# A layer of three mixers on one core: the attention's turn is given out in two parts, scores ahead of the heads' steps, values and transposes behind them

## The chip, the cores and the metric

The kernel runs on one core of a Trainium2 chip. The core has five engines with a queue of instructions each: TensorE (PE, matmuls and transposes, with a sequence of weight loads of its own, PEld), VectorE (DVE), ScalarE (ACT), GpSimd (POOL) and SyncE (SP, which issues DMAs). Operands lie in the on-chip memory SBUF, and results of matmuls in the accumulator memory PSUM. The metric is the device time of one execution in microseconds (us), less is better.

## The reference

One layer of a hybrid decoder trunk on 1024 positions of width 1024 in float32: a projection into three groups of columns, a mixer for each group, an output projection, then a gated MLP with a short convolution, a gated embedding and a last norm.

```python
z = rmsnorm(h, norm_mix_g[l]) @ w_in[l]
a_q, a_f, a_i, a_g, b_q, b_k, b_v, c_in = jnp.split(z, splits, axis=-1)
o_a = hgrn2_mix(a_q, a_f, a_i, a_g, lbs[l], hgrn_gnorm_g[l])
o_b = dilated_window_mix(b_q, b_k, b_v)
...
o_c, v_first = rwkv7_mix(c_in, ...)
h = h + jnp.concatenate([o_a, o_b, o_c], axis=-1) @ w_out[l]
h = h + conv_glu_ffn(rmsnorm(h, norm_ffn_g[l]), ...)
gate = jax.nn.sigmoid(rmsnorm(h, norm_ple_g[l]) @ ple_gate[l])
h = h + gate * (p[l] @ ple_proj[l])
```

Two of the mixers matter here. HGRN2 has four heads of 128 columns; in chunks of 64 positions it computes, for each head,

```python
o_inter = jnp.einsum('bhck,bhkv->bhcv', qc * jnp.exp(b), state)
scores = jnp.einsum('bhik,bhjk,bhijk->bhij', qc, kc, jnp.exp(rel))
o_intra = jnp.einsum('bhij,bhjv->bhiv', scores, vc)
state = (jnp.exp(b_last[:, :, 0, :])[..., None] * state
         + jnp.einsum('bhck,bhcv->bhkv', kc * jnp.exp(b_last - b), vc))
```

and norms the output per head. The attention has four heads of 64 columns and mixes three causal windows (128 positions, 512 with a stride of 4, 2048 with a stride of 16) by their softmax denominators; in the kernel that is one softmax over all earlier positions, with a mask that is added to the scores.

## The kernel before

The program is written stage by stage: norm and projection, RWKV-7, then the stage of this case with HGRN2 and the attention together, then the output projection, the MLP, the gated embedding and the last norm. In this stage several streams of work are Python generators. `phase_mix` (L321 to 341) writes an order as a list of letters, and `interleave` (L66) gives each letter's stream a turn up to its next `yield`:

- A and B are the HGRN heads. `handover` (L75) runs head 0 and then head 2 in A, head 1 and then head 3 in B. B starts six rounds after A.
- C is the attention, `swa` (L1110). It has a turn in the rounds of `TURNS`, two of three: 1, 3, 4, 6, 7, 9, 10, and so on to 33.
- F is `project_late` (L462): halves of the projections that are still due, 24 matmuls each (zp, L137 to 141), up to round 22, then the splitting of finished outputs into two parts for the output projection (L160, L162). It has a turn in the rounds of `LATE`: 1, 4, 7, 10, 13, 16, 19, 22 and then 23 to 28.
- M are 24 further pieces ahead of the first round.

One round is C, A, B, F, as far as each has a turn in it. A program that builds the kernel then arranges the instructions of each engine by readiness, with the written order as priority. So the written order is not quite the order on an engine. Engines wait for one another by semaphores.

A step of a head (`hgrn_head`, L950 to 1108): the head's inputs are loaded and prepared (L964 zl, L967 hk, L969 qt), own scores are made (L989), then come seven levels. A level is one step: 16 small matmuls (hsc, L1015) on the keys that ACT copied (ks, L1002); DVE copies them masked into hS (COPY_PREDICATED, L1017); keys and queries are multiplied by a factor (hk, L1026, on POOL in odd levels and DVE in even ones; qt, L1028, on DVE). The next level's matmuls need that qt and the next ks. After the levels come transposes of values and keys (vt, L1043 and L1049; ACT copies them to hV and hkt, L1044 and L1050), states (hkv, L1064, hst, L1071 and L1073), outputs (hpo, L1083 and L1085; ACT copies them to ho, L1086), the norm (square on ACT, hsq, L1090; sum on DVE, hss, L1092; power on POOL, hrs, L1095; product on DVE, ho, L1097), and transposes of the output (vt, L1103) with the gate (zl, L1104).

A turn of the attention handles one block of 128 queries (q block) of two heads. There are two pairs p of heads, of 8 q blocks each, and ten turns a pair, since the work is staggered:

- `swa_out` (L1215): after every fourth q block, the reciprocal denominators are spread by 16 matmuls (swd, L204) and the output ob multiplied (L1220);
- `swa_scores` (L1158) of q block qb: matmuls swq (L1169), a masked maximum on DVE (lg, L1179), the exponential on ACT (L1181);
- `swa_values` (L1199) of q block qb − 2: matmuls swo (L1209) on the transposed weights pT, and a copy to ob (L1210);
- `swa_turn` (L1186) of q block qb − 1: PE transposes the weights (swt, L1195), and ACT copies the first 512 columns of a head to pT, DVE the rest (L1196).

The later the q block, the more earlier positions it has, so that scores, values and transposes grow from turn to turn of a pair. PSUM holds four buffers of 512 columns, shared by hsc, vt, hkv, hpo, swt, swo, swd and zp, and two of 1024 columns for the scores swq, which the output projection (dp) uses after them.

Of the kernel before, what the change touches and what calls it, by code (L numbers as in the profile page):

```python
# [65 lines left out]
def interleave(order, streams):  # L66

    live = dict(streams)
    while live:
        for s in order:  # L70
            if s in live and next(live[s], STOP) is STOP:
                del live[s]


def handover(a, b, steps=14):  # L75

    for _ in range(steps):
        next(a)
        yield
    for i, _ in enumerate(b):  # L80
        if i == 1:
            for _ in a:
                yield
        yield
# [5 lines left out]
class Trunk:  # L90
# [231 lines left out]
    def phase_mix(self):  # L322
        nc, tc = self.nc, self.tc
        self.mix_norm()
        with tc.tile_pool(name="slots", bufs=1) as slots:
            self.slots, self.NSLOT = slots, 8
            self.rwkv()
        self.O, self.done = None, []
        for p in (0, 1):
            self.o_split(6 + p)  # L330
        with tc.tile_pool(name="hg", bufs=1) as slots, tc.tile_pool(name="sw", bufs=1) as sp:
            self.slots, self.NSLOT = slots, 11
            self.hgrn_setup()
            self.sp = sp
            self.swmask = sp.tile([P, T], F32, name="swmask")
            A = handover(self.hgrn_head(0), self.hgrn_head(2))
            B = handover(self.hgrn_head(1), self.hgrn_head(3))
            order = ["C", "A"] + ["M"] * 24
            for r in range(36):
                order += "C" * (r in self.TURNS) + "A" + "B" * (r > 5) + "F" * (r in self.LATE)  # L340
            interleave(order, {"A": A, "B": B, "C": self.swa(sp), "F": self.project_late(self.rest), "M": self.more})

    LATE = (1, 4, 7, 10, 13, 16, 19, 22, 23, 24, 25, 26, 27, 28)
# [766 lines left out]
    def swa(self, sp):  # L1110

        pend, fin, load = [], None, self.swa_load(sp, 0)
        self.nc.gpsimd.dma_start(self.swmask, self.a["swm"])
        yield
        for p in (0, 1):
            d = load
            self.swa_values_in(d)
            for qb in range(10):
                if fin:
                    self.swa_out(*fin)  # L1120
                    fin = None
                if qb < 8:
                    cur = self.swa_scores(sp, d, qb)
                if qb > 1:
                    fin = self.swa_values(sp, d, *pend.pop(0))
                if 0 < qb < 9:
                    pend[-1:] = [self.swa_turn(sp, *pend[-1])]
                if qb < 8:
                    pend.append((qb, *cur))
                if qb == 7 and p == 0:  # L1130
                    load = self.swa_load(sp, 1)
                yield
        self.swa_out(*fin)
# [735 lines left out]
```

## Time and profile before

| what | us |
|---|---|
| three runs | 1403.01, 1405.53, 1405.62 (median 1405.53) |
| span of the profiled execution | 1402.1 |
| time of the profiled execution outside the span | not given |
| hsc L1015, 16 matmuls, one level of one head | 0.69 busy |
| the stage of HGRN2 and the attention | about 384 to 568 |

The page of the profile gives the busy time of each engine over the span. A timeline gives instructions one by one: their start, their length, engine, line, operation, destination and sources; in brackets the time that the engine stood idle before it, and which instruction ended that. Equal neighbours are drawn together ("x16"). Matmuls overlap, so that the start of the next says better than a length how long PE was held. PE ran at the full clock (1.00) in the whole stage.

### The profile page before, as it was taken

The page shows a single profiled execution, that of the slowest core. Times are in us where ns is not written, and L with a number is a line of the kernel's source. Part 1 is how long each engine was busy: PE and PEld are TensorE (multiplying, and loading weights), DVE is VectorE, ACT ScalarE, POOL GpSimd, SP SyncE. Part 2 cuts the span into 40 slices and gives each one's busy share as a digit, 9 for nine tenths or more (in the row PEclk, how much of TensorE's full clock was granted, in tenths as well). Part 3 has the DMA queues.
Part 4 walks back from the last instruction along what each step waited for, and adds up shares of the span by engine and source line. Part 5 has one row for each costly group of instructions (what it writes and reads, how often), then busy time and mean ns, then how long its engine had stood idle before and what let it go on. Part 6 is the DMA issues. An engine that isn't in the chain of part 4 may idle for free.

```text
span 1402.1 us, 22348 instructions
## 1 busy us (share of the span) xinstructions
PE 1374.6 (98%) x8646; PEld 1115.5 (80%) x8646; DVE 1064.0 (76%) x1614; ACT 611.2 (44%) x1049; POOL 394.9 (28%) x286
## 2 busy tenths in 40 slices
PE   8999999999999999999999999999999999999997
PEld 6878777877878868788788888888888888888886
DVE  7696457845567796468889888888888799777685
ACT  7522323133255584255544343444344444455542
POOL 5421011201222242221245455445453000002342
PEclk9999999999999999999999999999999999999998
DMA  6123211322622211753233322232324963441334
GB/s 224 61 83 91 77 61 46 95 65 77 226 83 99 91 61 67 255 183 119 100 123 103 113 100 90 99 112 98 114 98 161 351 219 110 120 146 50 136 132 146
DMA packets 80122, 167.61 MB, mean 120 GB/s; under 512 B 19984, under 2 KB 22288, under 8 KB 80016
## 3 DMA queue, kind: packets, MB, share of 16 engines
q1 hardware_dynamic: 66784, 147.05, 31.0%
q10 hardware_dynamic: 12224, 15.47, 3.2%
q0 software_dynamic: 1008, 3.67, 0.7%
q8 instruction: 68, 1.11, 0.3%
q14 instruction: 38, 0.31, 0.1%
HBM read 119.76 MB, written 46.40 MB: 119 GB/s over the span
## 4 chain that ended last, share of the span: by engine, by line
PE 82%; DVE 6%; issue 6%; ACT 2%; POOL 2%; DMA 0%; SPq 0%; POOLq 0%; DVEq 0%; ACTq 0%
PE bg L1338 17%; PE bv L1338 13%; PE bv L1639 7%; PE bg L1639 7%; PE dp L137 7%; PE dp L139 7%; PE dp L141 7%; PE bv L137 1%; PE bv L141 1%; PE bv L139 1%; PE swq L1169 1%; PE hsc L1015 1%; PE bg L137 1%; PE bg L141 1%; PE bg L139 1%
## 5 line engine op out<-in xcount | busy, mean ns | idle before, releaser
L137 PE MATMUL dp<-xh,whi 128*128 128x512 f32 x544 | 186.6, 405 | 2.2 <-ACT xh L408 1.4
L139 PE MATMUL dp<-xl,whi 128*128 128x512 f32 x544 | 180.3, 393 | 0.8 <-DVE xl L409 0.6
L141 PE MATMUL dp<-xh,wlo 128*128 128x512 f32 x544 | 180.1, 393 | 0.4 <-POOL wlo L116 0.4
L116 POOL TENSOR_TENSOR wlo<-wraw,whi 128x512 fp32r<-128x512 f32 x60 | 83.6, 1395 | 267.1 <-ACT whi L114 216.4
L116 POOL TENSOR_TENSOR wlo<-raw,whi 128x512 fp32r<-128x512 f32 x84 | 134.9, 1625 | 75.8 <-ACT whi L114 75.8
L114 ACT CAST whi<-wraw 128x512 fp32r<-128x512 f32 x120 | 72.9, 617 | 161.4 <-PE dp L139 101.5
L1338 PE MATMUL bg<-t,whi 128*128 128x512 f32 x352 | 133.4, 389 | 0.0
L139 PEld LDWEIGHTS dp<-xl,whi 128*128 128x128 f32 x544 | 102.1, 188 | 25.1 <-DVE xl L409 3.0
L141 PEld LDWEIGHTS dp<-xh,wlo 128*128 128x128 f32 x544 | 102.2, 188 | 24.3 <-issue 2.0
L137 PEld LDWEIGHTS dp<-xh,whi 128*128 128x128 f32 x544 | 98.7, 189 | 26.5 <-issue 3.9
L116 POOL TENSOR_TENSOR wlo<-s,whi 128x512 fp32r<-128x512 f32 x44 | 64.6, 1468 | 168.6 <-ACT whi L114 168.6
L1639 PE MATMUL bg<-t,whi 128*128 128x512 f32 x308 | 95.1, 390 | 0.0
L1639 PE MATMUL bv<-t,whi 128*128 128x512 f32 x308 | 94.9, 389 | 0.0
L114 ACT CAST whi<-raw 128x512 fp32r<-128x512 f32 x88 | 52.7, 620 | 93.8 <-issue 48.6
L114 ACT CAST whi<-s 128x512 fp32r<-128x512 f32 x66 | 38.9, 620 | 120.2 <-PE bg L1338 112.8
L1338 PEld LDWEIGHTS bg<-t,whi 128*128 128x128 f32 x352 | 66.1, 188 | 13.8
L190 POOL TENSOR_TENSOR rst<-rst,mhalf 128x4 f32<-128x4 f32 (+1 forms) x9 | 10.2, 1133 | 233.4 <-DVE rst L186 218.0
L1338 PE MATMUL bg<-t,wlo 128*128 128x512 f32 x176 | 67.5, 389 | 0.0
L1639 PEld LDWEIGHTS bv<-t,whi 128*128 128x128 f32 x308 | 57.8, 188 | 12.0
L1639 PEld LDWEIGHTS bg<-t,whi 128*128 128x128 f32 x308 | 57.8, 188 | 11.8
L1635 ACT CAST t<-t 128x512 fp32r<-128x512 f32 x77 | 47.8, 622 | 43.9 <-PE bv L1639 28.1
L116 DVE TENSOR_TENSOR wlo<-wraw,whi 128x512 fp32r<-128x512 f32 x60 | 48.1, 806 | 20.9 <-ACT whi L114 18.6
(419 smaller groups left out, 3423.0 us busy)
## 6 DMA issues: line engine op xcount, KB each, us to landing
raw<-in_ffn_up_dram SPq DMA_DIRECT2D x44, 512.0 KB, 3.4
wraw<-in_w_in_dram SPq DMA_DIRECT2D x28, 512.0 KB, 3.3
z<-zst SPq DMA_DIRECT2D x18, 512.0 KB, 2.7
gb<-ct SPq DMA_DIRECT2D x33, 256.0 KB, 2.3
t<-gb SPq DMA_DIRECT2D x33, 256.0 KB, 2.8
t<-gt SPq DMA_DIRECT2D x33, 256.0 KB, 2.7
zl<-z SPq DMA_DIRECT2D x16, 512.0 KB, 4.5
wraw<-in_ple_gate_dram SPq DMA_DIRECT2D x16, 512.0 KB, 3.4
```

The costliest lines, as they stand in the source:

```text
L114: self.cast = nc.scalar.copy(hi, src).ins
L116: eng.tensor_tensor(lo, src, hi.bitcast(F32), ALU.subtract)
L137: nc.tensor.matmul(ps[hf], wh, xh[hf], start=first, stop=False)
L139: nc.tensor.matmul(ps[hf], wh, xl[hf], start=False, stop=False)
L141: self.step = nc.tensor.matmul(ps[hf], wl, xh[hf], start=False, stop=last).ins
L190: nc.gpsimd.tensor_tensor(r2, r, self.mhalf[:, :n], ALU.pow)
L1015: nc.tensor.matmul(sc[g:g + 64, c, :], ks[:, c * P + g:c * P + g + 64], x, start=True, stop=True)
L1169: m = nc.tensor.matmul(pq[h][:, b:b + w], d["q"][hs, qb * P:nk], d["k"][hs, b:b + w], start=True, stop=True)
L1338: nc.tensor.matmul(ps, w[part == 2][:, s], X[k][part == 1], start=start and k == part == 0, stop=k == 3 and part == 2, skip_group_check=no ...
L1635: nc.scalar.copy(xh, x)
L1639: nc.tensor.matmul(ps[m], wt[part == 2][:, m * P:(m + 1) * P], (xh, xl)[part == 1], start=k == part == 0, stop=k == NK - 1 and part == 2)
```

## The change

A turn of the attention gets a second `yield`. Its first part is the scores alone; the second part has everything else: the factor of a finished group of q blocks (`swa_out`), the values and the transposes. The order of a round gets the letter C a second time, behind A and B and ahead of F. Lines up to 339 keep their numbers, later ones move by one and, from the second hunk on, by two.

```diff
             for r in range(36):
-                order += "C" * (r in self.TURNS) + "A" + "B" * (r > 5) + "F" * (r in self.LATE)
+                turn = "C" * (r in self.TURNS)
+                order += turn + "A" + "B" * (r > 5) + turn + "F" * (r in self.LATE)
...
             for qb in range(10):
+                if qb < 8:
+                    cur = self.swa_scores(sp, d, qb)
+                yield
                 if fin:
                     self.swa_out(*fin)
                     fin = None
-                if qb < 8:
-                    cur = self.swa_scores(sp, d, qb)
                 if qb > 1:
                     fin = self.swa_values(sp, d, *pend.pop(0))
```

No instruction is added or taken away; those of the stage change places on PE, DVE, ACT and POOL. Three places follow.

**PE, rounds 5 and 6**, behind the projection block of round 4. Round 5 has no turn. hsc is a level of head 0, swo, swt and swq belong to the attention. Before:

```order
L141 MATMUL zp_4027<-xh_103,wlo_3910 128x512
L1015 MATMUL hsc_4054<-qt_3853,ks_4024 64x64 x8
L1209 MATMUL swo_4078<-pT_4002,sV_3855 64x128
L1209 MATMUL swo_4078<-pT_4007,sV_3855 64x128
...
L1195 MATMUL swt_4085<-cst,lg_3991 128x128 x3
L1195 MATMUL swt_4091<-cst,lg_3994 128x128 x3
L1169 MATMUL swq_4117<-zl_3737,zl_3735 128x512
L1169 MATMUL swq_4116<-zl_3737,zl_3735 128x512
L1169 MATMUL swq_4117<-zl_3737,zl_3735 128x128
L1169 MATMUL swq_4116<-zl_3737,zl_3735 128x128
L1015 MATMUL hsc_4096<-qt_3853,ks_4066 64x64 x8
```

With the change:

```order
L141 MATMUL zp_4027<-xh_103,wlo_3910 128x512
L1016 MATMUL hsc_4054<-qt_3853,ks_4009 64x64 x8
L1171 MATMUL swq_4117<-zl_3737,zl_3735 128x512
L1171 MATMUL swq_4116<-zl_3737,zl_3735 128x512
L1171 MATMUL swq_4117<-zl_3737,zl_3735 128x128
L1171 MATMUL swq_4116<-zl_3737,zl_3735 128x128
L1016 MATMUL hsc_4078<-qt_3853,ks_4066 64x64 x8
L1211 MATMUL swo_4097<-pT_4017,sV_3855 64x128
L1211 MATMUL swo_4097<-pT_4022,sV_3855 64x128
```

The values swo and the transposes swt, which stood between the two levels, now stand behind the second; between the levels only the scores are left.

**PE, rounds 20 and 21**, behind the projection block of round 19. hsc is a level of head 2; the attention is at the second pair. Before:

```order
L1015 MATMUL hsc_5042<-qt_4674,ks_4988 64x64 x8
L1169 MATMUL swq_5061<-zl_4541,zl_4539 128x512 x2
L1209 MATMUL swo_5070<-pT_4966,sV_4767 64x128
L1209 MATMUL swo_5070<-pT_4971,sV_4767 64x128
...
L1195 MATMUL swt_5077<-cst,lg_4955 128x128 x3
L1195 MATMUL swt_5083<-cst,lg_4958 128x128 x3
L1015 MATMUL hsc_5088<-qt_4674,ks_5054 64x64 x8
```

With the change:

```order
L1016 MATMUL hsc_5042<-qt_4674,ks_4973 64x64 x8
L1171 MATMUL swq_5123<-zl_4566,zl_4564 128x512
L1171 MATMUL swq_5122<-zl_4566,zl_4564 128x512
L1171 MATMUL swq_5123<-zl_4566,zl_4564 128x128
L1171 MATMUL swq_5122<-zl_4566,zl_4564 128x128
L1016 MATMUL hsc_5070<-qt_4674,ks_5054 64x64 x8
L1104 MATMUL vt_5091<-cst,ho_4924 128x128 x4
```

Again the scores alone are left between two levels; here they are those of q block 4 in place of q block 3, whose scores have gone ahead of the projection block.

**DVE, rounds 11 to 13.** hss and ho are the norm of head 0, pT the copies of transposed weights, hS and qt the level of head 1. Before:

```order
L1017 COPY_PREDICATED hS_4231<-cmask,hsc_4474 128x4x64
L1028 TENSOR_TENSOR qt_4169<-qt_4169,hT_4233 128x2x64x4
L1092 TENSOR_REDUCE hss_4549<-hsq_4547 128x8
L1196 COPY pT_4515<-swt_4522 128x384
L1196 COPY pT_4527<-swt_4534 128x384
L1093 TENSOR_SCALAR hss_4549<-hss_4549 128x8
L1017 COPY_PREDICATED hS_4231<-cmask,hsc_4555 128x4x64
L1097 TENSOR_TENSOR ho_4454<-ho_4454,hrs_4552 128x1024
L1028 TENSOR_TENSOR qt_4169<-qt_4169,hT_4233 128x2x32x8
```

With the change:

```order
L1018 COPY_PREDICATED hS_4231<-cmask,hsc_4474 128x4x64
L1029 TENSOR_TENSOR qt_4147<-qt_4147,hT_4233 128x2x64x4
L1093 TENSOR_REDUCE hss_4505<-hsq_4503 128x8
L1018 COPY_PREDICATED hS_4231<-cmask,hsc_4511 128x4x64
L1094 TENSOR_SCALAR hss_4505<-hss_4505 128x8
L1029 TENSOR_TENSOR qt_4147<-qt_4147,hT_4233 128x2x32x8
L1098 TENSOR_TENSOR ho_4454<-ho_4454,hrs_4508 128x1024
L1198 COPY pT_4540<-swt_4547 128x384
L1198 COPY pT_4552<-swt_4559 128x384
```

The two copies to pT, which stood ahead of the norm's product ho, now stand behind it.

## The prediction

> **What bounds the kernel now.** I read the page's busy times and the shares of the chain that ended last first.
>
> ```profile
> span 1402.1 us, 22348 instructions
> PE 1374.6 (98%) x8646; PEld 1115.5 (80%) x8646; DVE 1064.0 (76%) x1614; ACT 611.2 (44%) x1049; POOL 394.9 (28%) x286
> PE 82%; DVE 6%; issue 6%; ACT 2%; POOL 2%; DMA 0%; SPq 0%; POOLq 0%; DVEq 0%; ACTq 0%
> ```
>
> TensorE is busy 98% of the span. The change adds no matmul and takes none away, so it can only open or close gaps between matmuls. The stage that it touches runs from about 384 to 568 us. A table of busy time in four stretches of it comes next; after each stretch stand its length and the busy time of PE, weight loads, DVE, ACT and POOL.
>
> ```profile
> 384.00:434.00 50.00, 50.00 (x491) 37.81 (x490) 34.35 (x78) 29.61 (x68) 12.32 (x12) 1.00 0.19 63
> 434.00:484.00 50.00, 48.65 (x492) 40.96 (x490) 35.63 (x81) 22.82 (x52) 11.45 (x10) 1.00 0.32 109
> 484.00:534.00 50.00, 47.23 (x456) 35.94 (x456) 44.38 (x87) 39.34 (x74) 18.82 (x14) 1.00 0.22 73
> 534.00:568.00 34.00, 30.55 (x279) 25.82 (x278) 19.45 (x32) 11.52 (x21) 8.29 (x7) 1.00 0.30 105
> sum 184.00, PE 176.43 PEld 140.53 DVE 133.81 ACT 103.28 POOL 50.89; mean PE 44.11 PEld 35.13 DVE 33.45 ACT 25.82 POOL 12.72
> ```
>
> PE stands idle for 184.00 − 176.43 = 7.57 us in this stage: that is the most that any order of the same work can win, 0.54% of the span. Nothing of it lies in the first stretch. The timeline of PE shows where it is; in brackets stand the idle time and what ended it.
>
> ```profile
> 451.29 0.69 PE L1015 MATMUL hsc<-qt,ks 128*64 128x64 f32 x16 [0.59 <-ACT pT L1196]
> 452.52 0.50 PE L137 MATMUL zp<-xh,whi 128*128 128x512 f32 x1 [0.55 <-DVE pT L1196]
> 512.25 0.66 PE L1049 MATMUL vt<-cst,hk 128*128 128x128 f32 x4 [2.43 <-ACT hV L1044]
> 536.88 1.07 PE L1103 MATMUL vt<-cst,ho 128*128 128x128 f32 x8 [1.17 <-DVE ho L1097]
> 544.62 0.69 PE L1015 MATMUL hsc<-qt,ks 128*64 128x64 f32 x16 [0.44 <-DVE qt L1028]
> 562.13 1.06 PE L1103 MATMUL vt<-cst,ho 128*128 128x128 f32 x8 [1.77 <-DVE ho L1097]
> ```
>
> These six hold 6.95 of the 7.57 us. Only the first, second and fifth lie between level steps and attention work; the third and fourth hang on ACT and on a head's norm, and the last comes after the attention has ended.
>
> **The change part by part.** It moves; it adds and removes nothing. In a round with a turn, PE used to do scores, values and transposes, then step A, then step B. Now it does scores, A, B, values and transposes. What lies between one step of a head and its next is the cover under which its chain runs: hsc on PE, masked copy on DVE, factor on DVE (qt), next hsc on PE. Two thirds of the rounds have a turn, and a late projection block (24 matmuls, 5.5 us) lies ahead of the rounds without one, up to round 22. So the values and transposes move out of the passage from a round without a turn to the next, and into the passage that such a block covers already. That cover is lost at the former and of no use at the latter. The sum goes passage by passage.
>
> *Round 13 (a gain).* The transposes of q block 6, 16 matmuls, fill the four buffers that hsc and zp want too. In the first two rows of idle time above, hsc and zp wait for the copies that empty them. Now the hsc steps come ahead of the transposes and the values, and zp directly behind. Between transposes and zp nothing is left, but zp's first buffer is an older one. I take 0.59 + 0.55 = 1.1 us as won; the bounds are 0 (zp inherits the wait) and 1.1.
>
> *Round 5 to 6 (a loss).* In the order now, only the scores of q block 4 stand between two hsc of head 0.
>
> ```profile
> 404.78 0.69 PE L1015 MATMUL hsc<-qt,ks 128*64 128x64 f32 x16
> 405.29 0.61 PE L1209 MATMUL swo<-pT,sV 128*64 128x128 f32 x8
> 406.64 1.35 PE L1169 MATMUL swq<-zl,zl 64*128 64x512 f32 x8
> 407.92 0.69 PE L1015 MATMUL hsc<-qt,ks 128*64 128x64 f32 x16
> 405.85 1.33 DVE L1028 TENSOR_TENSOR qt<-qt,hT 128x512 f32<-128x512 f32 x1
> 409.12 0.68 DVE L1028 TENSOR_TENSOR qt<-qt,hT 128x512 f32<-128x512 f32 x1
> 405.36 1.27 POOL L116 TENSOR_TENSOR wlo<-wraw,whi 128x512 fp32r<-128x512 f32 x1 [4.16 <-ACT whi L114]
> ```
>
> From start to start, hsc holds PE for 405.29 − 404.78 = 0.51 us and the scores for 407.92 − 406.64 = 1.28. Values and transposes filled the 1.35 between. The factor ends at 407.18, 2.40 us after the hsc began; the cover left is 1.79, so PE waits 0.6. The factor took 1.33 us here against 0.68 in its other row, while a product of POOL ran beside it; if it took 0.68, the wait would be 0 (1.75 against 1.79). Bounds 0 and 0.6. I take 0.6, since POOL's product hangs on the projection's weights, which the change leaves in place. [...]
>
> *Rounds 12 and 13 (a loss).* Two things happen on PE and DVE.
>
> ```profile
> 442.97 0.69 PE L1015 MATMUL hsc<-qt,ks 128*64 128x64 f32 x16
> 443.48 1.48 PE L1209 MATMUL swo<-pT,sV 128*64 128x128 f32 x24
> 447.09 1.71 PE L1209 MATMUL swo<-pT,sV 128*64 128x128 f32 x28
> 476.62 0.70 PE L1169 MATMUL swq<-zl,zl 64*128 64x256 f32 x4
> 444.04 0.68 DVE L1028 TENSOR_TENSOR qt<-qt,hT 128x512 f32<-128x512 f32 x1
> 446.45 1.01 DVE L1196 COPY pT<-swt 128x384 f32<-128x384 f32 x2
> 449.31 1.23 DVE L1097 TENSOR_TENSOR ho<-ho,hrs 128x1024 f32<-128x1024 f32 x1 [1.43 <-POOL hrs L1095]
> 447.61 1.67 POOL L1095 TENSOR_TENSOR hrs<-hss,mhalf 128x8 f32<-128x8 f32 x1 [1.95 <-DVE hss L1093]
> ```
>
> First, the hsc at 442.97 is followed by the first two score blocks of the second pair. The larger takes 0.70, so I put both at 1.1 us together, and the next hsc could start at 444.58. Its factor ends at 444.72: 0.15 to 0.3 lost. Second, the copies of the transposed weights of q block 5 (pT, 1.01 us for two) used to stand ahead of the norm's product (ho) on DVE, and now stand behind it. That product waits for POOL's power until 449.28 and ends at 450.54. The first copy then ends near 450.9, 4.4 us later than the 446.45 + 0.5 at which it ended. PE wants it for the next values, which stood at 447.09; with scores gone ahead and the steps between, that demand comes at about 450.0. So PE waits 0.7 to 0.8. Together 1.0; bounds 0 (the scheduler's older pT would do) and 2.0 (both copies awaited, and the values' reading behind them).
>
> *Rounds 17 to 19 (a loss).* On ACT the copies of head 1's output now stand ahead of the copy that feeds a level's hsc (ks).
>
> ```profile
> 482.99 1.05 ACT L1086 COPY ho<-hpo 128x512 f32<-128x512 f32 x2
> ```
>
> At most that 1.05 is added, at least nothing; with a matmul block on either side I take 0.4.
>
> *Rounds 20 to 22 (a loss).* After the projection block of round 19, DVE is behind: the norm's product, the scaling of that block's result and the next head's preparation come before the level's factor.
>
> ```profile
> 490.99 1.13 PE L1169 MATMUL swq<-zl,zl 64*128 64x512 f32 x4
> 489.78 1.23 DVE L1097 TENSOR_TENSOR ho<-ho,hrs 128x1024 f32<-128x1024 f32 x1 [1.53 <-POOL hrs L1095]
> 492.25 0.69 DVE L320 TENSOR_TENSOR zp<-zp,rstd 128x512 f32<-128x512 f32 x1
> 493.18 0.68 DVE L1028 TENSOR_TENSOR qt<-qt,hT 128x512 f32<-128x512 f32 x1
> ```
>
> The factor ended at 493.86, some 3.5 us after its hsc had begun (0.62 ahead of 490.99). Scores, values and transposes covered that. Now the scores of q block 4 alone stand there, 1.28 us by the row of round 6, so the cover is 0.51 + 1.28 = 1.79 and the wait up to 1.7. As one of the preparing steps can be passed over, I take 1.0; bounds 0 and 1.7.
>
> *Rounds 23 to 28 (a loss).* The longest gap, 2.43 us behind ACT's burst, gets 0.4 more cover: the score block that stands in it has 896 columns in place of 768. The 0.44 near 544.6 goes, with transposes in front. Head 2's norm loses.
>
> ```profile
> 529.03 0.39 PE L1085 MATMUL hpo<-hst,qt 128*128 128x128 f32 x2
> 520.18 1.04 PE L204 MATMUL swd<-cst,sden 128*64 128x128 f32 x16
> 521.16 1.99 PE L1169 MATMUL swq<-zl,zl 64*128 64x512 f32 x8
> 523.07 1.31 PE L1209 MATMUL swo<-pT,sV 128*64 128x128 f32 x20
> 524.32 1.75 PE L1195 MATMUL swt<-cst,lg 128*128 128x128 f32 x12
> 535.50 1.22 DVE L1097 TENSOR_TENSOR ho<-ho,hrs 128x1024 f32<-128x1024 f32 x1 [1.53 <-POOL hrs L1095]
> ```
>
> Its chain took from 529.4 to 536.7. Between hpo and the transposes of its output there now stand two hsc and the four blocks shown, 1.0 + 0.98 + 1.9 + 1.25 + 1.6 = 6.7 us, so 0.7 would be bare even with the chain as it was. But its square and sum now stand behind that turn's copies on ACT and DVE, at most about 2 us (1.05 and 1.01 by the copies shown): the wait is 0.7 to 2.7, in place of 1.17. I take 2.6 there, hence +1.4 − 0.4 − 0.4 = 0.6; bounds −1.3 and +1.5.
>
> *The rest.* The last gap (1.77) lies behind the attention's end with the same chain ahead: 0. The second stretch has 1.35 idle, of which the first two rows take 1.14: elsewhere in it 0.2 can be won, and I take that.
>
> The sum: −1.1 + 0.6 + 1.0 + 0.4 + 1.0 + 0.6 − 0.2 = **+2.3 us**. The ends add up to −2.6 and +6.9. It is made against the profiled span, 1402.1 us; the page gives no other time for that execution, and the runs (1403.01 to 1405.62) are 0.9 to 3.5 above it. I add the sum to their median, 1405.53: **1407.8**.
>
> **The rivals.** *Gaps close and few open*: the scheduler hides what I count as lost. Then 1.1 + 0.2 + 0.4 + 0.4 go, and with head 2's 1.17, which would need its norm to run ahead of the copies, some 3.3 in all: 1402.2. For it speaks the first stretch, without a gap under the old order; against it, that its cover there is just what is taken away. *Heads' chain laid bare*: from the point where hsc and scores are shorter than hsc, masked copy and factor, 1.75 us at best (442.97 to 444.72) and 2.4 with POOL beside, each passage out of a round without a turn costs PE the rest, and a DVE operation in front (0.7 to 1.2 us) adds its own length. There are ten such passages in the stage up to round 33; at eight of them with 0.9 each the loss is 7.2: 1412.7. For it speaks the third stretch, where DVE is busy 44.38 of 50; against it, that later scores take up to 2 us and cover more. *Nothing changes*: the scheduler weighs the rows anew, and what PE loses at one place it has in store at the next: 1405.5. Against it speaks the order: hsc, scores, hsc stands there without anything between.
>
> **How the numbers follow.** Forecast 0.45 (own range 1405 to 1410.5), gaps close 0.21, chain laid bare 0.22, nothing 0.12. About 0.2%, 2.8 us, is what a measurement of this kernel can tell from no change: the bounds are 1402.7 and 1408.3. The forecast gives 0.27 same and 0.18 slower; nothing gives 0.11 same and 0.01 faster; gaps close 0.17 faster and 0.04 same; laid bare 0.22 slower. That makes faster 0.18, same 0.42, slower 0.40. The range cuts the far halves of both outer cases: 1401.5 to 1412.7.
>
> **What would show it.** In the changed trace: no wait ahead of hsc and zp near 451 (right for round 13); hsc near 407 waiting 0.6 for qt; values near 450 waiting for DVE's pT behind ho; hsc waiting for qt or zl near 492; the transposes of head 2's output waiting 2 us and more for ho. PE idle in the stage should be near 10 us. If it is under 7, the scheduler found cover that I did not see, and the passages from rounds without a turn will show no bracket; if it is over 13, the chain is bare at most of them. A change of PE's busy time outside the stage would make the whole sum wrong, as would a granted clock that differs from the 1.00 of these stretches.

## The result and the profile after

| | before | with the change |
|---|---|---|
| runs, us | 1403.01 to 1405.62, median 1404.74 of 4 | 1410.91, 1412.05, 1413.11, 1414.71, median 1412.58 |
| ratio, 95% interval | 1 | 1.0055 [1.0044, 1.0067] |
| span of the profiled execution, us | 1402.1 | 1411.3 |

The change costs 7.8 us, 0.55%: slower, inside the stated range by 0.1 us (its end is 1412.7), at the time of the rival in which the heads' chain is laid bare, and over three times what the forecast added. The page of the changed kernel, in the lines that were shown of before:

```profile
span 1411.3 us, 22341 instructions
PE 1376.2 (98%) x8646; PEld 1118.6 (79%) x8646; DVE 1066.7 (76%) x1614; ACT 611.3 (43%) x1049; POOL 392.4 (28%) x286
PE 81%; DVE 8%; issue 6%; ACT 2%; POOL 1%; DMA 0%; SPq 0%; POOLq 0%; DVEq 0%; ACTq 0%
```

Busy times of the engines hardly move; DVE's share of the chain that ended last goes from 6% to 8%. The table of busy time by stretches (length, PE, PEld, DVE, ACT, POOL, granted clock of PE, DMA share, GB/s) covers the longer stage:

```profile
384.00:434.00 50.00, 48.48 (x477) 36.45 (x475) 34.42 (x81) 28.06 (x65) 10.89 (x10) 1.00 0.17 59
434.00:484.00 50.00, 48.38 (x484) 40.33 (x483) 35.69 (x74) 22.02 (x44) 13.79 (x12) 1.00 0.28 101
484.00:534.00 50.00, 42.84 (x413) 34.50 (x413) 41.81 (x79) 36.68 (x72) 17.12 (x13) 0.97 0.27 85
534.00:578.00 44.00, 39.11 (x346) 32.69 (x345) 25.78 (x46) 16.22 (x31) 8.84 (x7) 0.96 0.19 63
```

PE is idle 15.2 us (194.00 − 178.81) where it was 7.57 (before has no wait between 568 and 578 us), and in the last two stretches the clock is 0.97 and 0.96 where it was 1.00 throughout. The timeline of PE names the waits, with the idle time and its end in brackets:

```profile
407.15 0.69 PE L1016 MATMUL hsc<-qt,ks 128*64 128x64 f32 x16 [0.58 <-DVE qt L1029]
446.39 0.69 PE L1016 MATMUL hsc<-qt,ks 128*64 128x64 f32 x16 [0.36 <-DVE qt L1029]
452.36 1.33 PE L1211 MATMUL swo<-pT,sV 128*64 128x128 f32 x12 [0.81 <-DVE pT L1198]
486.31 0.69 PE L1016 MATMUL hsc<-qt,ks 128*64 128x64 f32 x16 [0.29 <-ACT ho L1087]
496.81 0.69 PE L1016 MATMUL hsc<-qt,ks 128*64 128x64 f32 x16 [1.27 <-DVE qt L1029]
499.12 0.66 PE L1211 MATMUL swo<-pT,sV 128*64 128x128 f32 x8 [0.60 <-DVE zst L460]
505.93 0.66 PE L1197 MATMUL swt<-cst,lg 128*128 128x128 f32 x4 [0.75 <-ACT hS L1026]
507.18 0.47 PE L137 MATMUL zp<-xh,whi 128*128 128x512 f32 x1 [0.59 <-DVE hS L994]
517.07 0.66 PE L1050 MATMUL vt<-cst,hk 128*128 128x128 f32 x4 [1.18 <-ACT hV L1045]
522.57 0.70 PE L1016 MATMUL hsc<-qt,ks 128*64 128x64 f32 x16 [2.27 <-DVE qt L1029]
540.28 1.56 PE L1104 MATMUL vt<-cst,ho 128*128 128x128 f32 x8 [3.03 <-DVE ho L1098]
569.72 1.07 PE L1104 MATMUL vt<-cst,ho 128*128 128x128 f32 x8 [1.79 <-DVE ho L1098]
```

The two waits of round 13 (0.59 and 0.55, behind the transposes) are gone; the others are new or changed, but for the last, which was 1.77. The transposes behind that last wait start 7.6 us later than before (569.72 against 562.13).

The clock falls twice, by slices of one us (same columns; the clock is the third number from the end):

```profile
522.00:523.00 1.00, 0.43 (x14) 0.46 (x16) 1.00 (x5) 0.00 (x0) 0.00 (x0) 1.00 0.94 377
523.00:524.00 1.00, 1.00 (x23) 1.00 (x21) 1.00 (x6) 0.62 (x1) 0.00 (x0) 0.82 0.12 45
524.00:525.00 1.00, 1.00 (x9) 0.67 (x6) 0.85 (x2) 0.27 (x1) 0.00 (x0) 0.50 0.05 16
...
526.00:527.00 1.00, 1.00 (x6) 0.95 (x5) 0.48 (x3) 0.52 (x2) 0.00 (x0) 0.50 0.00 0
527.00:528.00 1.00, 0.93 (x8) 0.71 (x7) 1.00 (x3) 0.98 (x2) 0.00 (x0) 0.97 0.00 0
540.00:541.00 1.00, 0.72 (x6) 0.75 (x7) 1.00 (x3) 0.00 (x0) 0.00 (x0) 0.85 0.00 0
541.00:542.00 1.00, 1.00 (x8) 0.67 (x9) 1.00 (x3) 0.00 (x0) 0.00 (x0) 0.50 0.11 25
```

PE counts as busy there, but at half speed: from 523.6 to 527.1, and again for as long from 540.7 on. By the clock alone a stretch of 3.4 us at 0.50 does up to 1.7 us less work, an estimate from these rows. The gaps ahead of the two stretches were 2.27 and 3.03 us. Executions of one kernel differ in their clock: of the 61 runs of before that were timed beside the experiments, the five with a mean granted clock of 0.993 took 1405.4 us on average, and the ten with 0.996 or 0.997 took 1403.4.

Over the whole span the idle time of PE grew by 7.6 us (35.1 against 27.5, span less busy time) and its busy time by 1.6 (1376.2 against 1374.6); together that is the 9.2 us by which the span grew. By that estimate two half-clock stretches would lengthen the busy time by up to 3.4 us. Why only 1.6 came of it, these traces do not show.

### The profile page after: what moved, and what is told of

Read it like the earlier page. It is cut to its first block, busy times and chain, and to the rows that moved or that the text cites. A ratio compares the mean times of both kernels' runs of the same rounds, so it can differ in the third digit from the quotient of the medians.

```text
span 1411.3 us, 22341 instructions
## 1 busy us (share of the span) xinstructions
PE 1376.2 (98%) x8646; PEld 1118.6 (79%) x8646; DVE 1066.7 (76%) x1614; ACT 611.3 (43%) x1049; POOL 392.4 (28%) x286
## 4 chain that ended last, share of the span: by engine, by line
PE 81%; DVE 8%; issue 6%; ACT 2%; POOL 1%; DMA 0%; SPq 0%; POOLq 0%; DVEq 0%; ACTq 0%
PE bg L1340 17%; PE bv L1340 13%; PE bv L1641 7%; PE bg L1641 7%; PE dp L137 7%; PE dp L141 7%; PE dp L139 7%; PE bv L137 1%; PE bv L139 1%; PE bv L141 1%; PE bg L137 1%; PE bg L139 1%; PE bg L141 1%; DVE ig L585 1%; PE swt L1197 1%
```

## Experiments

Twelve kernels, each timed beside the kernel before on the same chip (its median 1404.6 to 1404.9 there). The theory at the start: values and transposes (the second part of a turn) gave cover between two steps of a head, and the change moves them to where it is of no use. The rivals: the scores' own new place; the place of the second part behind the heads' work on DVE and ACT; one section alone; the clock. "after" is the kernel with the change.

| kernel | median, us | ratio to before, 95% interval |
|---|---|---|
| e1_whole | 1405.29 | 1.0002 [0.9993, 1.0011] |
| e2_held | 1415.71 | 1.0079 [1.0065, 1.0093] |
| e3_upto21 | 1408.00 | 1.0024 [1.0015, 1.0032] |
| e4_from22 | 1409.59 | 1.0030 [1.0021, 1.0039] |
| e5_first | 1414.87 | 1.0072 [1.0059, 1.0086] |
| e6_second | 1414.98 | 1.0071 [1.0058, 1.0083] |
| e7_norm | 1413.40 | 1.0060 [1.0048, 1.0073] |
| e8_fill | 1412.44 | 1.0058 [1.0046, 1.0071] |
| e9_act | 1414.61 | 1.0075 [1.0062, 1.0087] |
| e10_before_act | 1402.68 | 0.9989 [0.9980, 0.9998] |
| e11_mirror | 1415.50 | 1.0081 [1.0067, 1.0094] |
| e12_late7 | 1408.36 | 1.0027 [1.0015, 1.0038] |

### Which part, and where

**e1_whole** gives out both parts together again:

```diff
-                order += turn + "A" + "B" * (r > 5) + turn + "F" * (r in self.LATE)
+                order += turn + turn + "A" + "B" * (r > 5) + "F" * (r in self.LATE)
```

> Both parts of a turn are given out together again, ahead of the heads' steps; of the change only one thing is left, that the scores come ahead of the factor of a finished group and not behind it. Theory (what is lost is the cover between two steps of a head, since values and transposes moved out of it): no loss, 1403.5 to 1406.5 us, PE idle in the stage 7 to 9 us and no half-clock stretch. Rival (the loss comes from the scores' own new place, or from any new order that the scheduler meets): slower by 4 us or more.

No loss: 1405.3 us, with PE idle for 8.6 us in the stage. That the scores now come ahead of `swa_out` costs nothing; the loss lies in the split. One thing was not expected: the profiled execution has a half-clock stretch from 512.8 us, behind a wait of 2.41.

**e3_upto21** and **e4_from22** split the turn in one section only (shown for the first):

```diff
+                ahead, back = ("", turn) if r < 22 else (turn, "")
+                order += turn + ahead + "A" + "B" * (r > 5) + back + "F" * (r in self.LATE)
```

> The turn is split up to round 21 alone; from round 22 both parts stand ahead of the heads' steps. Theory (many passages lose a little): the idle time of PE that the changed kernel gained up to 500 us stays, some 3.7 us, and what it gained after 505 us goes; 1407 to 1410 us, no half-clock stretch. Rival (the end of the stage alone carries the loss): 1404 to 1406 us.

> The turn is split from round 22 on alone. Theory: what the changed kernel lost after 505 us stays, 1.3 + 2.4 us of idle time and 1.5 to 3 us for two stretches at half the clock: 1408 to 1412 us. Rival (the loss at the end follows from the lateness that the earlier rounds bring): 1404 to 1406 us.

Both lose: +3.3 and +4.9 us, together 8.1 against the 7.8 of the whole change. So the loss is spread over these two sections, and theirs add up to it; both rivals, which put all of it into one, fall. The runs of e4_from22 spread from 1405.74 us at a mean clock of 0.996 to 1410.70 at 0.992, so part of its loss is clock. The first keeps every wait of after up to 500 us (0.58, 0.36, 0.81, 0.29, 1.27, 0.60) and has no half-clock stretch in the stage. The second has half-clock stretches from 515 and from 536 us, behind a wait for ACT's burst and behind the wait for head 2's norm:

```profile
513.79 0.66 PE L1051 MATMUL vt<-cst,hk 128*128 128x128 f32 x4 [1.52 <-ACT hV L1046]
535.53 1.50 PE L1105 MATMUL vt<-cst,ho 128*128 128x128 f32 x8 [3.02 <-DVE ho L1099]
```

The 3.02 was 1.17 before, as in the first of the two kernels (1.18).

### Is it lost cover

**e2_held** keeps the split but holds the second part back into the round without a turn, where the scores had been left alone:

```diff
+                back = "C" * (r % 3 != 1 and r > 1)
+                order += turn + "A" + "B" * (r > 5) + back + "F" * (r in self.LATE)
```

> The turn stays split and the second part stays behind the heads' steps, but in rounds ahead of a projection block it is held back into the next round, the one without a turn. So values and transposes lie between two steps of a head again where the scores stood alone, and no longer beside the projection block. Theory (lost cover): the waits before hsc near 407, 446 and 497 us go, and with them most of the loss; PE idle in the stage 6 to 10 us, time 1403 to 1407 us. Rival (values, transposes and their copies behind the heads' work on DVE and ACT are the cost, wherever there is cover): the time stays at 1410 us or more.

**e5_first** and **e6_second** split every other turn up to round 21, so that one passage is restored and another thinned (`r % 3 == 0` and `r % 3 == 1`).

> Split alone in the turns of rounds 3, 6, 9 to 21, which follow a round without a turn; the other turns whole, ahead of the heads' steps. If the passage out of a round without a turn is the place of the loss up to round 21, the waits before hsc near 407 and 497 us stay and the time is 1406.5 to 1408.5 us. If any passage with scores alone is, the loss is shared with the next kernel, about half of the 3.3 us in each.

> Split alone in the turns of rounds 4, 7, 10 to 19, so that values and transposes stand directly ahead of a projection block and the passage out of a round without a turn keeps its whole turn; scores alone stand in the passage one round later. If only the passage out of a round without a turn loses, 1403.5 to 1405.5 us and no wait near 407 and 497. If scores alone are too little cover anywhere, 1406 to 1408 us, with waits of hsc for qt one round later.

All three miss, and the theory with them, as far as it promised a cure: none is faster than after (their intervals overlap with its own, that of e2_held only just). Each of e5_first and e6_second loses some 10 us, though e3_upto21, which splits the turns of both, loses 3.3: inside this section the losses do not add up. In e2_held the waits near 407 and 446 us are gone, as the theory has it, but at 451 us there is a longer one, and the one near 497 grew from 1.27 to 2.06. All in all PE is idle for less than in after, 12.7 us in the stage against 15.2, though not for the 6 to 10 expected. But 13.6 us of the stage are at half the clock (3.4 from 452, 6.8 from 500 and 3.4 from 520 us) where after has 6.8, and PE's busy time is 1379.6 us against 1376.2. So what the cover won in idle time was lost again in busy time. e5_first, which still has 0.58 near 407, has the same one, and e6_second waits for a factor instead:

```profile
451.14 0.98 PE L1198 MATMUL swt<-cst,lg 128*128 128x128 f32 x7 [3.51 <-ACT ob L1213]
```

```profile
452.38 0.98 PE L1198 MATMUL swt<-cst,lg 128*128 128x128 f32 x7 [3.95 <-ACT ob L1213]
504.36 0.97 PE L1017 MATMUL hsc<-qt,ks 128*64 128x64 f32 x16 [2.84 <-DVE qt L1030]
```

```profile
455.44 1.00 PE L1017 MATMUL hsc<-qt,ks 128*64 128x64 f32 x16 [3.23 <-DVE qt L1030]
```

The long waits stand beside a head's norm and the next head's preparation (rounds 12 and 13, and 19 to 21).

**e11_mirror** splits the other way round, values and transposes ahead of the heads' steps and scores behind:

```diff
-                if qb < 8:
-                    cur = self.swa_scores(sp, d, qb)
-                yield
...
+                yield
                 if qb < 8:
-                    pend.append((qb, *cur))
+                    pend.append((qb, *self.swa_scores(sp, d, qb)))
```

> The turn is split the other way round: factor, values and transposes ahead of the heads' steps, scores behind them. If it is the place of values and transposes that costs: 1403 to 1407 us and the waits of the changed kernel near 407, 497 and 522 us absent. If two parts with heads' steps between cost by themselves, or the scores' place counts: 1409 us or more.

It is as slow as e2_held, +10.9 us. Transposes now follow close behind their own exponential, and wait 4.37 us for it near 455. So the place of values and transposes is not all; any split tried so far costs.

### DVE's queue, the norm, the clock

**e7_norm** gives the norm (square, sum, scale, power) the priority that the scores have, in after:

```diff
+        with self.tc.high_priority(offset=4000):
+            nc.scalar.activation(sq, o, AF.Square)
...
```

> The changed kernel, with the priority of the scores given to each head's norm as well (square on ACT, sum and scale on DVE, power on POOL). Theory (head 2's norm waits 3.0 us because its square and sum stand behind copies that wait for PE): the wait before the transposes near 540 us falls under 1.5 us, the half-clock stretch behind it goes, 1408.5 to 1411 us. Rival (the norm's own length is bare since the work that covered it moved): the wait stays over 2.5 us and the time at 1412 us or more.

Undecided between the two: the wait for head 2's output falls from 3.03 to 1.65 and the half-clock stretch behind it goes (clock 1.00 from 540 to 550 us), so the norm's place in the queues was a cause; but 0.59 and 0.77 appear behind it, in rounds 26 to 28, and the time stays, at 1413.4.

**e8_fill** fills that wait with work that does nothing; the result of the added transposes is overwritten:

```diff
+            for c in range(20 if h == 2 and not hf else 0):
+                nc.tensor.transpose(pt[:, :P], self.ident, self.ident)
```

> The changed kernel with 20 transposes of a constant added ahead of the transposes of head 2's output; their result is overwritten. They take about 2.3 us of PE in the gap of 3.0. Theory (an idle stretch of PE of this length calls a stretch of some 3.4 us at half the clock, which costs 1.7 us): the stretch near 540 us goes though 20 instructions are added, 1410 to 1412 us. Rival (the stretch has another cause and hides nothing): it stays, and the time is 1412.5 us or more.

```profile
540.00:541.00 1.00, 1.00 (x16) 0.83 (x16) 1.00 (x2) 0.00 (x0) 0.00 (x0) 1.00 0.00 0
541.00:542.00 1.00, 1.00 (x30) 1.00 (x26) 1.00 (x3) 0.56 (x1) 0.00 (x0) 1.00 0.20 29
```

```profile
539.72 1.09 PE L1106 MATMUL vt<-cst,ho 128*128 128x128 f32 x8 [0.60 <-DVE ho L1098]
543.87 2.26 PE L1199 MATMUL swt<-cst,lg 128*128 128x128 f32 x14 [1.14 <-DVE zl L1107]
548.27 1.75 PE L1213 MATMUL swo<-pT,sV 128*64 128x128 f32 x28 [1.37 <-DVE pT L1200]
```

With 0.60 us left of the gap of 3.03 the clock stays at 1.00, where it fell to 0.50 in after: between these two kernels the stretch went with the idle time. The runs agree, with a mean clock of 0.995 to 0.997 in all five against 0.992 to 0.995 in the four of after. Yet the time is that of after, 1412.4: PE, after a wait of only 0.60 and at full speed, now waits 1.14 and 1.37 us for DVE a few blocks later. As far as this run tells, the slow clock was no loss of its own in this section; DVE was late anyway.

**e9_act** and **e10_before_act** move all pT copies to ACT, in after and in before:

```diff
-                (nc.vector.tensor_copy if b else nc.scalar.copy)(t[:, b:b + w], pt[:, :w])
+                nc.scalar.copy(t[:, b:b + w], pt[:, :w])
```

> The changed kernel with all copies of transposed weights on ACT; some 7.5 us of copies leave DVE (two of 0.28, 0.42, 0.50 and 0.68 us in each pair). Theory (values and transposes behind the heads' steps meet a DVE queue that is late with the heads' factors and norms, and PE waits for that queue): the waits for qt and pT shrink, 1407.5 to 1410.5 us. Rival (PE lacks work at those places whatever DVE does, or ACT's queue is as late): 1411.5 us or more.

> The kernel before with the same copies on ACT, as a measure for the last run. If DVE's queue costs only where its cover was lost: within 1.5 us of the kernel before, 1403.5 to 1406 us. If DVE's load costs everywhere: 1400 to 1403 us.

After gains nothing and rather loses (1.0075 against 1.0055, with intervals that just overlap), against the theory. Before gains 2 us, 0.11%, as it should if DVE's load costs everywhere: the two waits of round 13 shrink to one of 0.28. e10_before_act is the fastest kernel of the study and beats both. e9_act shows what a wait of 3.5 to 4 us near 451 us is. The timelines of DVE, ACT and POOL in e9_act, around that wait (PE stands until 452.09, 3.94 us, for the first ob):

```profile
446.55 1.66 POOL L1096 TENSOR_TENSOR hrs<-hss,mhalf 128x8 f32<-128x8 f32 x1 [1.16 <-DVE hss L1094]
448.24 1.22 DVE L1098 TENSOR_TENSOR ho<-ho,hrs 128x1024 f32<-128x1024 f32 x1 [1.77 <-POOL hrs L1096]
449.38 1.22 DVE L1181 CUSTOM_DVE_ANT_0 lg<-swq,swmask 128x1024 f32<-128x1024 f32 x1
450.64 1.15 ACT L1183 ACTIVATE lg<-lg,sden 128x1024 f32<-128x1024 f32 x1 [4.00 <-DVE sden L1181]
451.79 0.24 ACT L1212 COPY ob<-swo 128x128 f32<-128x128 f32 x1
```

It is read from the bottom: PE wants a PSUM buffer that ob frees; ob stands on ACT behind an exponential, that waits for the maximum on DVE, the maximum stands behind the norm's product, and the product waits for POOL. In e5_first the chain is the same; in e2_held and e11_mirror the next head's preparation stands between product and maximum as well (2.9 and 2.1 us from the end of the one to the start of the other). The scores are those of q block 7, 1024 columns. In before and after they come ahead of the projection block of round 10, and their exponentials end at 435.8 and 440.0 us, before the norm; in e2_held, e5_first, e9_act and e11_mirror they come behind it.

**e12_late7** tests that alone, in before: those scores lose their priority, and three of their four matmuls fall behind the block.

```diff
-                        order.enter_context(self.tc.high_priority(offset=4000))
+                        if qb != 7 or d["p"]:
+                            order.enter_context(self.tc.high_priority(offset=4000))
```

> The kernel before, in which the scores of q block 7 of the first pair alone lose their priority, so that three of their four matmuls fall behind the projection block of round 10, beside head 0's norm, as the whole of them did in the kernels e2_held, e5_first, e9_act and e11_mirror, which all waited 3.5 to 4.4 us near 448 to 455 us. Theory (the copy that frees a PSUM buffer stands on ACT behind the exponential, that behind the maximum on DVE, that behind the norm's product, and that waits for POOL): a wait of 2.5 to 4.5 us there in this kernel too, perhaps a half-clock stretch behind it, 1407 to 1410 us. Rival (those waits come from values and transposes behind the heads' steps): none over 1.2 us there, 1403.5 to 1406 us.

```profile
446.95 0.55 PE L1196 MATMUL swt<-cst,lg 128*128 128x128 f32 x3 [0.77 <-ACT ob L1211]
448.87 1.18 PE L1169 MATMUL swq<-zl,zl 64*128 64x128 f32 x8 [0.76 <-DMA zl<-z]
```

The time comes out as expected, +3.8 us, but not by the expected wait. ob is late by the same chain up to the maximum, but the maximum comes ahead of the norm's product here and does not wait for POOL: 0.77 us. The rest is other waits (0.76 for a load; 1.70 us near 516) and two half-clock stretches. So one block of scores in another place, with no split, costs half of what the change costs; that it makes the 3.5 us by itself is not shown.

## Why the prediction held, and where it was off

That the time fell inside the range, at 1412.58 of 1412.7, is luck in part: two of the four runs lie above its end, and the forecast's own range (1405 to 1410.5) was missed. The direction was right, and most of the terms came true, in place, in cause and nearly in size (idle time of PE, after less before):

| term | forecast, us | measured, us |
|---|---|---|
| round 13, behind the transposes | −1.1 | −1.14 |
| round 5 to 6 | +0.6 | +0.58 (hsc waits for qt, 1.32 long beside a product of POOL again) |
| rounds 12 and 13 | +1.0 | +1.17 (0.36 for qt, 0.81 for pT) |
| rounds 17 to 19 | +0.4 | +0.29 (hsc waits for the copy ho itself, which empties a PSUM buffer, and not for a ks behind it) |
| rounds 20 to 22 | +1.0 | +1.7 (1.27 for qt, 0.60 for a buffer, small ones against each other) |
| burst, head 2's norm, the 0.44 | −0.4 + 1.4 − 0.4 | −1.25 + 1.86 − 0.44 |

These forecasts sum to 2.5 and the measured ones to 2.8. The step that failed is "The rest": it said that the passages not listed could only win 0.2. They lost, some 4.7 us in sum. Four small waits up to 471 us came to some 1.1 more than before, and 1.34 us stand near 506, ahead of and behind the transposes. The largest is the 2.27 near 522.6, in rounds 23 and 24. In part it is the forecast's own mechanism, not looked for there: between two levels of one head there stood 6.8 us of PE's work before (519.65 − 512.84 by the starts of hsc), with values, transposes and scores among it; now there stands one block of states, and the factor is late on DVE. Before:

```profile
512.84 0.89 PE L1015 MATMUL hsc<-qt,ks 128*64 128x64 f32 x16
519.65 0.70 PE L1015 MATMUL hsc<-qt,ks 128*64 128x64 f32 x16
514.52 0.67 DVE L1028 TENSOR_TENSOR qt<-qt,zl 128x512 f32<-128x512 f32 x1
516.20 0.67 DVE L1026 TENSOR_TENSOR hk<-hk,hT 128x512 f32<-128x512 f32 x1
```

With the change:

```profile
517.65 0.88 PE L1016 MATMUL hsc<-qt,ks 128*64 128x64 f32 x16
518.47 1.83 PE L1065 MATMUL hkv<-hV,hkt 128*128 128x128 f32 x14
518.31 1.58 DVE L1027 TENSOR_TENSOR hk<-hk,hT 128x512 f32<-128x512 f32 x1
520.80 1.62 DVE L1029 TENSOR_TENSOR qt<-qt,zl 128x512 f32<-128x512 f32 x1
517.61 1.73 POOL L162 TENSOR_TENSOR xl<-oc,xh 128x512 fp32r<-128x512 f32 x1
520.73 1.15 POOL L1027 TENSOR_TENSOR hk<-hk,hT 128x512 f32<-128x512 f32 x1 [1.39 <-ACT ks L1003]
```

Two more things stand in the rows. The product of the keys (hk), which came behind it on DVE, now comes ahead of it; and both products run beside one of POOL and take 1.58 and 1.62 us where they took 0.67, as the forecast had it for rounds 5 and 6 alone. These 1.9 us are most of the wait, by an estimate from the rows; that POOL's products cause them is not shown, since no run here takes those away.

The second error is the clock, which was taken as 1.00 throughout; the prediction named that as a thing that would make its sum wrong. Two stretches stand for up to 3.4 us by the estimate above, though in e8_fill the time stayed when one of them was gone.

Against the cases: the rival that lays the chain bare gave 1412.7 with eight passages of 0.9; the time agrees, the picture only in part, since the waits are fewer and longer at the end, and part of the time is clock. "Nothing changes" and "gaps close" fall. The expected PE idle time of about 10 us (over 13: the chain is bare at most places) came out at 15.2.

What the forecast's reason does not carry is a cure. It read the loss as cover moved from where it is needed; e2_held put the cover back there, had less idle time than the change and was no faster. Shown is: the split causes the loss (e1_whole), by two sections that add up (e3_upto21, e4_from22), while the turns of the first do not (e5_first, e6_second). In the traces each new order meets the queues of DVE and ACT at a head's norm in another place. Open is whether a split exists that loses nothing; the six other splits of the table (e2 to e6 and e11) were all slower than before.

## What to carry to other kernels

Where PE is 98% busy and the rest of its time hangs on queues of other engines, price a move by each passage between two dependent matmuls, all of them, and not by those that look worst before: what stands between them against the chain on the other engines, with what is queued ahead on DVE and ACT at that moment. A copy that frees a PSUM buffer can be part of PE's path (PE stood 3.94 us for one in e9_act), so look at what it stands behind.

## What the runs showed that was not expected

- PE's clock fell to 0.50 in the middle of a busy kernel, for 3.4 us (after) or twice that (6.8 from 500 us in e2_held), behind idle time of 1.5 us in two pieces (e12_late7, 0.77 and 0.76 within 3 us), of 2.27 and of 3.03 us (after). It did not do so each time: behind a gap of 2.43 us in before the clock stayed at 1.00, behind one of 2.41 in e1_whole at the same place it fell (columns of the second row as above):

```profile
512.33 0.70 PE L1050 MATMUL vt<-cst,hk 128*128 128x128 f32 x4 [2.41 <-ACT hV L1045]
512.81:516.22 3.41, 3.41 (x37) 2.93 (x36) 3.34 (x7) 3.28 (x6) 1.80 (x2) 0.50 0.58 169
```

What decides between the two is not shown. So what a gap cost could not be told from its length alone. With the gap of 3.03 us filled up to 0.60, no slow stretch followed (e8_fill).

- A slow stretch need not cost its estimated 1.7 us: taking one away in e8_fill gained nothing (1412.44 against 1412.58), since PE then waited 1.14 and 1.37 us for DVE.
- Moving 7.5 us of copies from DVE to ACT gained 0.11% under the old order and nothing under the new one (1414.61 against 1412.58): the same edit is worth something else under another order of the same work.
